# First modulation wholly on TensorE, gate1 loads earlier, paired head products, filler products

## The chip, the cores and the metric

The kernel runs on one core of one Trainium2 chip. The metric is device time in microseconds (us). Before the change three runs gave a median of 1546.49 us (1546.27 to 1547.13).

## What is computed

One layer of a hybrid encoder block on x of 512 tokens by 1024 channels, float32, with one conditioning vector c:

```python
mod = silu(c) @ w_ada + b_ada
shift1, scale1, gate1, shift2, scale2, gate2 = split(mod, 6)
h = rms_norm(x) * (1 + scale1) + shift1
q, k, v, zg = split(h @ w_in)
attn = windowed_gqa(q, k, v, sink)        # 8 heads, 2 kv heads, blocks of 128, band of 3 blocks
u, vg = split(gelu(zg), 2)
gm = u * (W_s @ layer_norm(vg) + b_s)     # per chunk of 128 tokens, 8 channel groups
mix = concat(rms_norm(attn), rms_norm(gm))
x = x + gate1 * rms_norm(mix @ w_out)
h2 = rms_norm(x) * (1 + scale2) + shift2
# expert choice: 16 experts, each takes its 64 best tokens of softmax(h2 @ w_router)
out_e = (silu(xs @ w_gate) * (xs @ w_up)) @ w_down   # 1024 -> 2816 -> 1024, times the gate
x = x + gate2 * rms_norm(scatter_add(out_e))
```

The three expert weights are 16 x 3 x 11.5 MB = 554 MB and are read once.

## The kernel before

The program has two parts. The **mixing part** computes everything up to the routing; the **expert part** runs sixteen experts one after the other on weights that stream from HBM. All transfers are issued on SP's queue, in program order, and an issue that must wait for its buffer holds up all issues behind it. The Tile framework's planner puts each engine's instructions in an order at build time; on the chip each engine then runs its own list strictly in that order.

Stages of the mixing part, in program order:

- **Loads**: small vectors, x, then eight `wq` chunks of 1.4 MB, one for each block of 128 channels: the columns of `w_ada` for shift1 and scale1 of these channels, and the rows of `w_in` for q, k, v.
- **x**: squares on ScalarE, 32 transposes (`x_cols`), 1/rms with `rsqrt` (a guess from the bits and three Newton steps on VectorE, eight instructions for a single column), 1/rms as a row (`x_norm`, `rxb`).
- **q, k, v**: the order of `SEQ`, with `m` = the first modulation's shift1 and scale1 of a channel block, `d` = `modulate` (two VectorE passes and one on ScalarE give h in two float32r parts), `q` = `qkv` (18 products of 512 columns into the six banks `qkp`). For the blocks in `MODPE` (0, 1, 2, 3, 5) `m` is `mod1_rows`, 32 products on TensorE; for blocks 4, 6 and 7 it is `mod1_acc`, eight VectorE passes, and `mod1_cols` at `d` finishes it with a few products.
- **g units**: eight `unit("g", k)` of 12 products, for the gMLP's v half. Beside them `mod2(0, *)` and `mod2(1, *)`: each `mod2(i, kk)` loads 1 MB of `w_ada` into a slot and adds two row tiles to `racc` with two VectorE passes (L553, L555); i = 0 is gate1, 1 shift2, 2 scale2, 3 gate2. `mod2_cols(i)` then makes columns on TensorE, and for gate1 spreads it over 128 rows (`G0`, 16 products).
- **u units**: eight `unit("u", k)`, for the u half. Beside them `mod2_cols(0)`, `mod2_cols(1)`, `mod2(2, *)`, and `gate_norm(b)` for each token block: layer norm of v, with an `rsqrt` of its own, then two GpSimd passes.
- **steps** (`at_step`, one for a head pair of a block): `attn_scores`, two steps later `attn_out`, which transposes the probabilities of heads j and j + 4 and multiplies them with v, 128 columns to a product (L462, two to six products a head); the spatial gating, the split of `w_out` into two parts (`out_weights`, L656/L657), the output projection (`project`, `project_z`), `residual`, then for each token block `x2_cols`, `logits`, `affinity`, and for the last block the routing of the first expert (`rank_part`, `route(0)`). `gate2` (step `GS` = 23) spreads gate2 over 128 rows.

Expert chunks go to buffers that the mixing part frees: six slots, three buffers that held `wz` (parts of `w_out`, last read by `project_z(3, 1)`), three that lie where the attention's tiles were, one where `ow` was, and places. The loads of the first expert's weights wait for them (L835).

The six slots also hold `wq`, `ada2`, `wst`, part of `wi` and `wo`. `load_gu("u", 0)` goes to a place that `xT` held and so waits for the last `modulate`.

Of the kernel before, what the change touches and what calls it, by code (L numbers as in the profile page):

```python
# [7 lines left out]
F32 = mybir.dt.float32  # L8
# [6 lines left out]
P = 128  # L15
# [9 lines left out]
NE = 16  # L25
# [22 lines left out]
TINY = 2.0 ** -126  # L48


@with_exitstack
def encoder_block(ctx, tc, x, c, w_ada, b_ada, norm_pre_mix, norm_post_mix, w_in, sink, sgu_ln_g,
# [32 lines left out]
    # ---------------------------------------------------------------- loads  # L85
# [17 lines left out]
    # columns of w_ada for shift1, scale1 of 128 channels with the rows of w_in for q, k, v of these channels  # L103
# [18 lines left out]
    def more_loads():  # L122
# [15 lines left out]
        nc.sync.dma_start(lnb, sgu_ln_b.to_broadcast([P, DG]))  # L138
        wst = slot([NG, P], name="wst")
# [4 lines left out]
    # ---------------------------------------------------------------- constants  # L144
# [24 lines left out]
    def make_dist():  # L169
        """|distance|, or a huge number outside the window; keys in front of, of, behind the block"""  # L170
# [10 lines left out]
    def rsqrt(dst, v, n):  # L181
        """dst = 1/sqrt(v) for [P, n] f32, to f32's accuracy: a guess from the bits, then Newton."""
        i = rs.tile([P, n], I32, name="rs_i", tag=f"rs_i{min(n, 2)}", bufs=2 if n == 1 else 1)
        nc.vector.tensor_scalar(i, v.bitcast(I32), -0.5, float(0x5F3759DF), op0=OP.mult, op1=OP.add)
        h = rs.tile([P, n], F32, name="rs_h", tag=f"rs_h{min(n, 2)}", bufs=2 if n == 1 else 1)
        nc.vector.tensor_scalar(h, v, -0.5, None, op0=OP.mult)
        y = i.bitcast(F32)
        t = rs.tile([P, n], F32, name="rs_t", tag=f"rs_t{min(n, 2)}", bufs=2 if n == 1 else 1)
        for r in range(3):
# [5 lines left out]
            o = dst if r == 2 else rs.tile([P, n], F32, name="rs_y", tag=f"rs_y{min(n, 2)}")  # L195
            nc.vector.scalar_tensor_tensor(o, t, 1.5, y, op0=OP.add, op1=OP.mult)
            y = o
# [29 lines left out]

    param_cols(0, np0)
# [8 lines left out]
    # ---------------------------------------------------------------- x: transposed; 1 / rms  # L237
# [29 lines left out]
    # ---------------------------------------------------------------- shift1, scale1; h  # L267
# [7 lines left out]
    def mod_rows(pm, col, w, n, first, last):  # L275
        """w [P, 4, n]: four column tiles of the array add col^T w at once"""
# [4 lines left out]
    def mod_cols(rows, n):  # L281
        """the four rows of rows [P, n] as columns: [P, n / 128, 4] in PSUM"""
# [5 lines left out]
    def mod1_rows(k):  # L288
        """PE: even and odd rows of w_ada in column tiles of their own"""
# [17 lines left out]
    acc1 = {}  # L307

    def mod1_acc(k):
        """DVE: the sums over a partition's rows"""  # L310
        acc1[k] = t = ea.tile([P, 2, P], F32, name="acc1", bufs=2)
        for kk in range(KD):
            w = wq[k][0][:, :, kk]
            if kk == 0:
                nc.vector.tensor_scalar(t, w, cs[:, kk:kk + 1], None, op0=OP.mult)
            else:
                nc.vector.scalar_tensor_tensor(t, w, cs[:, kk:kk + 1], t, op0=OP.mult, op1=OP.add)  # L317

    def mod1_cols(k):
        pm = bank("pm")  # L320
        for j in range(2):
            nc.tensor.matmul(pm[32 * j:32 * j + 32, :P], ones.to_broadcast([P, 32]), acc1[k][:, j], start=True,
                             stop=True, tile_position=(0, 32 * j))
        rows = rs.tile([P, P], F32, name="rows", bufs=1)[:64]
        nc.vector.tensor_copy(rows, pm[:64, :P])
        pt = bank("pt")
        nc.tensor.transpose(pt[:, :64], rows, ident[:64, :64])
        mod1_end(k, pt[:, 0:1], pt[:, 32:33])

# [6 lines left out]
    # ---------------------------------------------------------------- input projection  # L336
# [3 lines left out]
    def split(hi, lo, src):  # L340
        """src as a sum of two parts that float32r holds"""
# [10 lines left out]
    def qkv(k):  # L352
        """heads j and j + 4 of q share a block of rows; then k, v"""
# [10 lines left out]

    for b in range(NB):
        sumsq(ssx[:, b:b + 1], x_sb[:, b], junk)
        if b == NB - 1:
            x_rsqrt(b, NB)
        x_cols(b)
        if b == NB - 2:  # L370
            x_rsqrt(0, b + 1)
    def emit(what, k):
        if what == "m":
            (mod1_rows if k in MODPE else mod1_acc)(k)
        elif what == "d":
            if k not in MODPE:
                mod1_cols(k)
            modulate(k)
        elif what == "q":
            if k == KD - 1:  # L380
# [5 lines left out]
                load_gu("g", 0)  # L386
            qkv(k)
            if k == 0:
                more_loads()
                load_gu("g", 1)  # L390

# [49 lines left out]

    def attn_out(n, j):
        """the same heads' outputs, transposed"""
        k0, k1 = max(0, n - 1), min(NB, n + 2)
        w = (k1 - k0) * P
        if j == 0 or (n, j) == (NB - 1, 3):
            po[n, j] = bank("po")
        else:
            po[n, j] = po[n, 0]
        pT = []  # L450
        for g in range(2):
            pt = bank("ptr")
            for i in range(k1 - k0):
                nc.tensor.transpose(pt[:, i * P:(i + 1) * P], probs[n, j][:, g, i * P:(i + 1) * P], ident)
            pT.append(at.tile([P, 3 * P], F32, name="pT", tag="pT", bufs=4))
# [629 lines left out]
```

## Time and profile before

| | us |
|---|---|
| median of three runs | 1546.49 |
| span of the profiled execution | 1544.5 |
| first expert product (L949) begins | 266.5 |
| TensorE busy in the span | 1387.1 |
| VectorE busy in the span | 429.7 |

The page names 596.86 MB of transfers, 386 GB/s over the span. No execution time of the profiled run is given apart from its span, which is 2.0 us under the median of the runs. [...]

### The profile page before, as it was taken

Reading aid. Unit: us, or ns where it says so; the run is one execution under the profiler, and the core shown is the slowest. Engines: PE = TensorE matmul, PEld = TensorE weight load, DVE = VectorE, ACT = ScalarE, POOL = GpSimd, SP = SyncE. Lnnn points to the kernel's source line nnn. Section 1 sums busy time; section 2 is a strip of 40 time slices with the busy share of each in tenths; the row PEclk is TensorE's granted clock in tenths of the full one; section 3 lists DMA queues with packets and bytes.
Section 4 is the critical chain, followed back from the end, with each engine's and each line's share of the span. In section 5 each row is a group of like instructions: output and inputs, shape, how many; then the busy total and the mean of one; then the engine's idle time right before and its main releaser. Section 6 shows DMA issues by size and latency. Waiting matters only on the chain.

```text
span 1544.5 us, 17570 instructions
## 1 busy us (share of the span) xinstructions
PE 1387.1 (90%) x7282; PEld 619.8 (40%) x7282; DVE 429.7 (28%) x1087; ACT 188.9 (12%) x404; POOL 116.0 (8%) x144
## 2 busy tenths in 40 slices
PE   7888998999999998998898998989898989898986
PEld 5665665343444433333333333324242423333323
DVE  5789857112112120212112111112020303020104
ACT  3336433000010000000100000000000000000001
POOL 2457310000000000000000000000000000000002
PEclk9998999999999999999999999999999999999998
DMA  9776608999999999999999999999999999999995
GB/s 316 275 252 181 241 6 334 415 411 428 429 429 429 429 429 428 429 428 429 429 428 429 429 429 429 429 428 429 429 428 429 429 429 429 428 429 429 429 396 202
DMA packets 92711, 596.86 MB, mean 386 GB/s; under 512 B 8692, under 2 KB 31960, under 8 KB 44760
## 3 DMA queue, kind: packets, MB, share of 16 engines
q1 hardware_dynamic: 92632, 595.74, 93.3%
q8 instruction: 57, 0.93, 0.2%
q14 instruction: 22, 0.18, 0.0%
HBM read 593.62 MB, written 2.10 MB: 386 GB/s over the span
## 4 chain that ended last, share of the span: by engine, by line
DMA 60%; PE 28%; DVE 8%; issue 1%; ACT 1%; POOL 1%; SPq 0%; DVEq 0%; ACTq 0%; POOLq 0%
DMA w<-in_w_down_dram 23%; DMA w<-in_w_up_dram 19%; DMA w<-in_w_gate_dram 18%; PE pf L949 11%; PE pd L991 4%; PE px L888 1%; PE pys L1001 1%; PE py L348 1%; PE py L346 1%; PE po L462 1%; PE py L347 1%; DVE ex L851 1%; PE pd L1031 1%; DVE racc L555 1%; DVE acc L317 1%
## 5 line engine op out<-in xcount | busy, mean ns | idle before, releaser
L949 PE MATMUL pf<-w,ex 128*64 128x512 f32 (+1 forms) x3072 | 638.0, 561 | 42.0 <-DMA w<-in_w_up_dram 40.6
L949 PEld LDWEIGHTS pf<-w,ex 128*64 128x64 f32 x3072 | 215.0, 137 | 433.2 <-issue 326.2
L991 PE MATMUL pd<-w,ex 128*64 128x512 f32 (+1 forms) x1440 | 319.3, 563 | 33.7 <-DMA w<-in_w_down_dram 33.7
L991 PEld LDWEIGHTS pd<-w,ex 128*64 128x64 f32 x1440 | 109.9, 136 | 231.7 <-issue 126.0
L967 DVE TENSOR_TENSOR ex<-pf,ex 128x512 f32<-128x512 f32 (+1 forms) x48 | 30.4, 647 | 362.3 <-PE pf L949 362.0
L995 DVE TENSOR_SCALAR ex<-pd,gc 128x512 f32<-128x512 f32 x15 | 11.3, 751 | 377.6 <-PE pd L991 377.6
L907 POOL COPY ex<-ex 128x512 f32<-128x512 f32 x16 | 9.8, 613 | 1138.2 <-DVE ex L905 1058.0
L888 PE MATMUL px<-x_sb,ex 128*64 128x256 f32 x512 | 71.0, 386 | 8.6 <-DVE ex L864 7.4
L919 ACT ACTIVATE ex<-pot 128x512 f32<-128x512 f32 x16 | 9.6, 597 | 544.6 <-PE pot L917 544.6
L1007 DVE TENSOR_TENSOR y<-pys,y 128x512 f32<-128x512 f32 x112 | 68.2, 681 | 17.0 <-PE pys L1001 17.0
L974 ACT ACTIVATE ex<-pht 128x512 f32<-128x512 f32 (+1 forms) x48 | 23.5, 559 | 374.6 <-PE pht L973 374.6
L1001 PE MATMUL pys<-ex 64*128 64x512 f32 x240 | 55.6, 602 | 12.7 <-DVE ex L995 12.7
L900 DVE TENSOR_SCALAR ex<-pxt,mods 128x64 f32<-128x64 f32 x128 | 34.9, 337 | 92.0 <-PE pxt L895 92.0
L888 PEld LDWEIGHTS px<-x_sb,ex 128*64 128x64 f32 x512 | 41.3, 136 | 38.3 <-DVE ex L864 18.8
L851 DVE SCALAR_TENSOR_TENSOR ex<-rt,afs,before 128x512 f32<-128x512 f32 (+2 forms) x65 | 46.8, 719 | 12.3 <-PE rt L858 12.3
L913 DVE COPY gc<-pgc 128x1 f32<-128x1 f32 x16 | 2.5, 158 | 152.6 <-PE pgc L910 152.6
L555 DVE SCALAR_TENSOR_TENSOR racc<-ada,cs,racc 128x1024 f32<-128x1024 f32 x28 | 42.6, 1521 | 0.2
L959 ACT ACTIVATE ex<-pf 128x512 f32<-128x512 f32 (+1 forms) x48 | 26.9, 561 | 121.2 <-PE pf L949 120.4
L1001 PEld LDWEIGHTS pys<-ex 64*128 64x128 f32 x240 | 21.9, 186 | 47.1 <-DVE ex L995 25.9
L973 PE MATMUL pht<-ident,ex 128*128 128x128 f32 x176 | 25.7, 295 | 12.1 <-DVE ex L967 12.1
L973 PEld LDWEIGHTS pht<-ident,ex 128*128 128x128 f32 x176 | 22.7, 213 | 22.7 <-DVE ex L967 22.7
L890 ACT ACTIVATE ex<-px 128x256 f32<-128x256 f32 x32 | 12.3, 383 | 125.7 <-PE px L888 125.6
(254 smaller groups left out, 1086.3 us busy)
## 6 DMA issues: line engine op xcount, KB each, us to landing
w<-in_w_gate_dram SPq DMA_DIRECT2D x128, 1408.0 KB, 26.8
w<-in_w_up_dram SPq DMA_DIRECT2D x126, 1408.0 KB, 26.8
w<-in_w_down_dram SPq DMA_DIRECT2D x120, 1408.0 KB, 26.8
ada<-in_w_ada_dram SPq DMA_DIRECT2D x16, 1024.0 KB, 6.5
w<-in_w_down_dram SPq DMA_DIRECT2D x18, 512.0 KB, 9.6
wq<-in_w_ada_dram SPq DMA_DIRECT2D x16, 512.0 KB, 5.9
wi<-in_w_in_dram SPq DMA_DIRECT2D x4, 1024.0 KB, 5.2
wq<-in_w_in_dram SPq DMA_DIRECT2D x8, 384.0 KB, 6.2
```

The source lines that it names most:

```text
L555: nc.vector.scalar_tensor_tensor(acc[i], t[:, r], cs[:, k:k + 1], acc[i], op0=OP.mult, op1=OP.add)
L851: nc.vector.scalar_tensor_tensor(junk[:, :c1 - c0], p[:, c0:c1], afs[:, b, e:e + 1], before[:, o + c0:o + c1], op0=OP.subtract, op1=OP.is_ ...
L888: nc.tensor.matmul(px[i][h * CAP:(h + 1) * CAP, :256], ohr[:, b], x_sb[:, b, c0:c0 + 256], start=(b == 0), stop=(b == NB - 1))
L900: nc.vector.tensor_scalar(xs[:, k], pt[:, c0:c0 + CAP], s2[:, k:k + 1], sh2[:, k:k + 1], op0=OP.mult, op1=OP.add)
L949: nc.tensor.matmul(pb[n][h * 64:(h + 1) * 64, :NW[n]], XS[e][:, k], t, start=(i == 0), stop=(i == KD - 1))
L959: nc.scalar.activation(hid[:, n * 512:n * 512 + NW[n]], pg[n][:, :NW[n]], AF.Silu)
L967: nc.vector.tensor_tensor(hs, pu[n][:, :NW[n]], hs, op=OP.mult)
L973: nc.tensor.transpose(p[:, j * P:(j + 1) * P], hv[:, j0 + j], ident)
L974: nc.scalar.activation(hT[:, j0:j0 + n], p.rearrange("p (j t) -> p j t", j=4)[:, :n], AF.Copy)
L991: nc.tensor.matmul(pd[dh * 64:(dh + 1) * 64, c0:c0 + n], hT[:, j, h * CAP:(h + 1) * CAP], t[:, o - q * FF:o - q * FF + n], start=(h == 0 a ...
L1001: nc.tensor.matmul(p, OT[e][dh * 64:(dh + 1) * 64, b * P:(b + 1) * P], oe[dh * 64:(dh + 1) * 64, :], start=True, stop=True)
L1007: nc.vector.tensor_tensor(yb, p, yb, op=OP.add)
```

## The change

- `mod1_acc`, `mod1_cols` and `MODPE` go; `mod1_rows` does all eight blocks.
- In `SEQ` gate1's four loads and eight VectorE passes (`a0` to `a3`) stand among the last `m`, `d`, `q`; the g loop then takes `mod2(1, *)` and `mod2(2, *)`, with `mod2_cols(0)` after g unit 2; `mod2_cols(1)` and `mod2_cols(2)` stand in the u loop after units 0 and 3. gate2's loads stay at steps 8 and 9, its columns go from step 10 to 11. `M2` and `GN` go.
- `load_wst` is moved behind `q2`, `load_gu("g", 0)` from `q7` to `q3`, `load_gu("g", 1)` from `q0` to `q6`.
- `attn_out` gathers heads j and j + 1 in one `pT` tile per group and multiplies both at once, 256 columns to a product, at odd j. `pT` has two buffers of twice the size, where it had four.
- `rsqrt` takes minus half of its argument and has one third-order step and one Newton step: six instructions for one column, eight for several (eight and eleven before). The callers form minus half of the argument in an instruction that they had already. `x_rsqrt` runs once for all four blocks; `gate_norm` runs once, with one `rsqrt` of four columns.
- `keep_warm`: products into a bank that nobody reads: six of 512 columns ahead of `param_cols(0)`; for the last token block one of 256 behind each half of `x2_cols`, three of 256 behind `logits`; four of 128 in `route(0)`.
- `gate2` moves from step 23 to 20. The last block's projection is cut 2 + 2 heads where it was 3 + 1.

```diff
-MODPE = (0, 1, 2, 3, 5)
-SEQ = "d0 m1 q0 d1 m2 d2 m3 q1 d3 m4 q2 d4 m5 q3 d5 m6 q4 d6 m7 q5 d7 q6 q7"
-M2 = (0, 0, 1, 1, 3)
-M3 = (8, 8, 9, 9, 10)
-GN = (None, None, 0, 0)
-GS, RS = 23, 21
+SEQ = "d0 m1 q0 d1 m2 d2 m3 q1 d3 m4 q2 d4 m5 q3 d5 m6 q4 d6 m7 a0 q5 d7 a1 q6 a2 q7 a3"
+M3 = (8, 8, 9, 9, 11)
+GS, RS = 20, 21
...
-    def rsqrt(dst, v, n):
+    def rsqrt(dst, h, n):
         i = rs.tile([P, n], I32, name="rs_i", tag=f"rs_i{min(n, 2)}", bufs=2 if n == 1 else 1)
-        nc.vector.tensor_scalar(i, v.bitcast(I32), -0.5, float(0x5F3759DF), op0=OP.mult, op1=OP.add)
-        h = rs.tile([P, n], F32, name="rs_h", tag=f"rs_h{min(n, 2)}", bufs=2 if n == 1 else 1)
-        nc.vector.tensor_scalar(h, v, -0.5, None, op0=OP.mult)
+        nc.vector.tensor_scalar(i, h.bitcast(I32), -0.5, GUESS, op0=OP.mult, op1=OP.add)
...
+        square()
+        p = rs.tile([P, n], F32, name="rs_p", tag=f"rs_y{min(n, 2)}")
+        nc.vector.scalar_tensor_tensor(p, t, 5 / 3 / ALPHA ** 2, t, op0=OP.add, op1=OP.mult)
+        z = rs.tile([P, n], F32, name="rs_y", tag=f"rs_y{min(n, 2)}")
+        nc.vector.scalar_tensor_tensor(z, p, 1.25 / ALPHA ** 4, y, op0=OP.add, op1=OP.mult)
+        y = z
+        square()
+        nc.vector.scalar_tensor_tensor(dst, t, 1.5, y, op0=OP.add, op1=OP.mult)
...
+    def keep_warm(w, data, n):
+        p = bank("warm")
+        for _ in range(n):
+            nc.tensor.matmul(p[:, :data.shape[1]], w, data, start=True, stop=True)
+
+    keep_warm(before[:, :P], before[:, :S], 6)
     param_cols(0, np0)
...
         if what == "m":
-            (mod1_rows if k in MODPE else mod1_acc)(k)
+            mod1_rows(k)
         elif what == "d":
-            if k not in MODPE:
-                mod1_cols(k)
             modulate(k)
...
+            elif k == 2:
+                load_wst()
+            elif k == 3:
+                load_gu("g", 0)
+            elif k == 6:
                 load_gu("g", 1)
+        else:
+            mod2(0, k)
...
         for g in range(2):
+            if j % 2 == 0:
+                pTs[g] = at.tile([P, 3, 2, P], F32, name="pT", tag="pT", bufs=2)
             pt = bank("ptr")
...
+        if j % 2:
+            for i in range(nk):
+                for g in range(2):
+                    nc.tensor.matmul(po[n, j][g * HD:(g + 1) * HD, (j - 1) * P:(j + 1) * P],
+                                     v_sb[:, k0 + i, g * HD:(g + 1) * HD], pTs[g][:, i].rearrange("p j q -> p (j q)"),
+                                     start=(i == 0), stop=(i == nk - 1))
...
-        mod2(k // 4, k % 4)
+        mod2(1 + k // 4, k % 4)
+        if k == 2:
+            mod2_cols(0)
...
-        if k < 2:
-            mod2_cols(k)
-        if GN[k] is None:
-            gate_norm(k)
+        if k in (0, 3):
+            mod2_cols(1 + k // 3)
+        if k == 0:
+            gate_norm()
```

## Rows read from the trace of the kernel before

**Rows 1.** The page's 40 slices of the span: DMA busy, in tenths.
```profile
DMA  9776608999999999999999999999999999999995
```
**Rows 2.** Windows by stage: fields as told under the profile before.
```profile
16.00:70.00 54.00, 47.69 (x304) 34.90 (x304) 34.84 (x71) 17.73 (x31) 18.78 (x24) 0.91 0.87 282
70.00:93.50 23.50, 23.32 (x102) 18.54 (x102) 15.91 (x12) 7.19 (x12) 15.15 (x10) 1.00 0.97 355
93.50:131.00 37.50, 32.72 (x152) 22.53 (x150) 37.30 (x77) 13.56 (x26) 22.79 (x16) 0.91 0.63 193
131.00:154.50 23.50, 17.92 (x161) 10.71 (x161) 21.16 (x49) 17.98 (x39) 16.30 (x20) 0.91 0.57 176
154.50:231.80 77.30, 74.86 (x433) 53.05 (x432) 53.75 (x176) 31.33 (x82) 16.88 (x27) 0.94 0.34 123
231.80:247.40 15.60, 15.43 (x95) 11.44 (x94) 11.23 (x48) 7.18 (x21) 0.93 (x2) 1.00 0.99 403
247.40:266.60 19.20, 11.94 (x103) 8.41 (x104) 14.37 (x67) 6.60 (x18) 0.61 (x1) 0.91 0.72 284
266.60:1522.00 1255.40, 1146.77 (x5824) 448.23 (x5824) 221.15 (x528) 75.20 (x151) 14.22 (x19) 1.00 1.01 425
```
**Rows 3.** Waits of SP's queue, 184 to 233 us: us in total, times, longest.
```profile
SPq L835 <- PE py L348: 49.2, 2, 48.8
```
**Rows 4.** Waits of TensorE, 0 to 266 us, same columns.
```profile
PE pm L322 <- DVE acc L317: 4.5, 2, 2.6
PE ptr L454 <- DVE am L432: 4.1, 2, 3.7
...
PE po L462 <- ACT pT L459: 3.2, 7, 1.4
...
PE pm L278 <- DVE racc L555: 2.8, 1, 2.8
```
**Rows 5.** Timeline of VectorE: start, us, instruction; x's rsqrt, then `residual`'s.
```profile
12.61 0.14 DVE L258 TENSOR_SCALAR ssx<-ssx 128x1 f32<-128x1 f32 x1
...
15.77 0.68 DVE L196 SCALAR_TENSOR_TENSOR rx<-rs_t,rs_y 128x1 f32<-128x1 f32 x1
...
250.18 0.15 DVE L184 TENSOR_SCALAR rs_i<-vv 128x1 int32<-128x1 int32 x1
...
251.74 0.16 DVE L196 SCALAR_TENSOR_TENSOR rr<-rs_t,rs_y 128x1 f32<-128x1 f32 x1
```
**Rows 6.** Timeline of TensorE: the first modulation's two forms; idle time and releaser in brackets.
```profile
41.30 0.41 PE L322 MATMUL pm<-acc,ones 128*32 128x128 f32 x4 [1.90 <-DVE acc L317]
...
42.74 1.08 PE L293 MATMUL pm<-wq,cs 128*32 128x128 f32 x32
```
**Rows 7.** Windows of 4 us around the second fall of the clock, fields as in Rows 2.
```profile
52.00:56.00 4.00, 2.27 (x10) 1.46 (x11) 3.46 (x11) 0.00 (x0) 0.26 (x1) 0.86 1.06 406
56.00:60.00 4.00, 4.00 (x15) 3.17 (x13) 2.67 (x6) 1.49 (x3) 0.74 (x1) 0.71 0.96 387
```
**Rows 8.** Waits of SP's queue, 40 to 64 us.
```profile
SPq L119 <- DVE t L332: 11.5, 1, 11.5
```
**Rows 9.** Timeline of VectorE: passes of `mod2` beside the g units and later.
```profile
74.73 13.73 DVE L555 SCALAR_TENSOR_TENSOR racc<-ada,cs,racc 128x1024 f32<-128x1024 f32 x7
...
166.59 1.27 DVE L555 SCALAR_TENSOR_TENSOR racc<-ada,cs,racc 128x1024 f32<-128x1024 f32 x1
```
**Rows 10.** Timeline of TensorE: head outputs, and the routing at the end of the part.
```profile
207.36 0.87 PE L462 MATMUL po<-pT,v_sb 128*64 128x128 f32 x10
...
220.54 0.66 PE L462 MATMUL po<-pT,v_sb 128*64 128x128 f32 x8 [1.45 <-ACT pT L459]
...
252.83 1.93 PE L712 MATMUL ph<-ident,x_sb 128*128 128x128 f32 x8 [3.79 <-DVE x_sb L698]
...
258.25 2.03 PE L585 MATMUL spr<-ident,mods 128*128 128x128 f32 x16
...
261.63 4.06 PE L888 MATMUL px<-x_sb,ex 128*64 128x256 f32 x32 [1.24 <-DVE rank L872]
```

More of the change, by code (lines that the diff above doesn't have):

```diff
@@ L305, in mod1_end @@
         nc.vector.tensor_tensor(sh1[:, k:k + 1], shift, pcol("ba", k), op=OP.add)
[L307 to L328, printed above, removed]
     def modulate(k):
@@ L363, in qkv, with mod2 @@
             mm3(qkp[m], h[:, c0:c0 + P], l[:, c0:c0 + P], hh[k], hl[k], k == 0, k == KD - 1)
+    G0 = cp.tile([P, D], F32, name="G0")
+    mods = cp.tile([P, 4, 8], F32, name="mods")
+    g1c, sh2, s2, g2c = (mods[:, i] for i in range(4))
+    rb = cp.tile([P, NE], F32, name="rb")
+    acc = {}
+    def mod2(i, kk):
+        t = slot([2, D], name="ada2")
+        nc.sync.dma_start(t, ada[:, 2 * kk:2 * kk + 2, 2 + i])
+        if kk == 0:
+            acc[i] = (ea if i < 2 else at).tile([P, D], F32, name="racc")
+        for r in range(2):
+            k = 2 * kk + r
+            if k == 0:
+                nc.vector.tensor_scalar(acc[i], t[:, r], cs[:, k:k + 1], None, op0=OP.mult)
+            else:
+                nc.vector.scalar_tensor_tensor(acc[i], t[:, r], cs[:, k:k + 1], acc[i], op0=OP.mult, op1=OP.add)
@@ new lines, in mod2_cols @@
+    def mod2_cols(i):
+        pm = bank("pm2")
+        mod_rows(pm, ones, acc[i].rearrange("p (j w) -> p j w", j=4), 256, True, True)
+        rows = at.tile([P, 256], F32, name="rows2", tag="pT", bufs=2)
+        nc.vector.tensor_copy(rows, pm[:, :256])
+        m = mod_cols(rows, 256)
+        nc.vector.tensor_tensor(mods[:, i].rearrange("p (j q) -> p q j", j=4), m,
+                                pcol("ba", 16 + 8 * i, 8).rearrange("p (j q) -> p q j", j=4), op=OP.add)
+        if i == 0:
+            nc.vector.tensor_tensor(g1c, g1c, pcol("pom", 0, 8), op=OP.mult)
+            spread(G0, g1c)
+        elif i == 2:
+            nc.vector.tensor_tensor(s2, s2, pcol("npf", 0, 8), op=OP.mult)
+            pb = bank("pb")
+            for k in range(KD):
+                mod_rows(pb, sh2[:, k:k + 1], wr[:, k:k + 1].to_broadcast([P, 4, NE]), NE, k == 0, k == KD - 1)
+            nc.vector.tensor_scalar(rb, pb[:, :NE], -1.0, None, op0=OP.mult)
+            nc.vector.scalar_tensor_tensor(wsp[:, :, :NE], wr, -1.0, s2.unsqueeze(2).to_broadcast([P, KD, NE]),
+                                           op0=OP.mult, op1=OP.mult)
+        elif i == 3:
+            nc.vector.tensor_tensor(g2c, g2c, pcol("pof", 0, 8), op=OP.mult)
@@ L365, in encoder_block, with spread @@
+    def spread(dst, cols):
+        for i in range(2):
+            p = bank("spr")
+            for k in range(4):
+                kk = i * 4 + k
+                nc.tensor.matmul(p[:, k * P:(k + 1) * P], cols[:, kk:kk + 1].to_broadcast([P, P]), ident,
+                                 start=True, stop=True)
+            nc.scalar.activation(dst[:, i * 512:(i + 1) * 512], p, AF.Copy)
     for b in range(NB):
@@ L534, in gmlp_cols @@
         nc.vector.tensor_tensor(ml, p, mh.bitcast(F32), op=OP.subtract)
-    G0 = cp.tile([P, D], F32, name="G0")
-    mods = cp.tile([P, 4, 8], F32, name="mods")
-    g1c, sh2, s2, g2c = (mods[:, i] for i in range(4))
-    rb = cp.tile([P, NE], F32, name="rb")
-    acc = {}
-    def mod2(i, kk):
-        t = slot([2, D], name="ada2")
-        nc.sync.dma_start(t, ada[:, 2 * kk:2 * kk + 2, 2 + i])
-        if kk == 0:
-            acc[i] = (ea if i < 2 else at).tile([P, D], F32, name="racc")
-        for r in range(2):
-            k = 2 * kk + r
-            if k == 0:
-                nc.vector.tensor_scalar(acc[i], t[:, r], cs[:, k:k + 1], None, op0=OP.mult)
-            else:
-                nc.vector.scalar_tensor_tensor(acc[i], t[:, r], cs[:, k:k + 1], acc[i], op0=OP.mult, op1=OP.add)
@@ L579, in spread @@
-    def spread(dst, cols):
-        for i in range(2):
-            p = bank("spr")
-            for k in range(4):
-                kk = i * 4 + k
-                nc.tensor.matmul(p[:, k * P:(k + 1) * P], cols[:, kk:kk + 1].to_broadcast([P, P]), ident,
-                                 start=True, stop=True)
-            nc.scalar.activation(dst[:, i * 512:(i + 1) * 512], p, AF.Copy)
     pacc = {}
@@ L764, in encoder_block @@
         at_step(OWS[k], (out_weights, k))
-        at_step(M2[k], (mod2, 2, k))
         at_step(M3[k], (mod2, 3, k))
-    at_step(M2[4], (mod2_cols, 2))
     at_step(M3[4], (mod2_cols, 3))
-    for k in range(4):
-        if GN[k] is not None:
-            at_step(GN[k], (gate_norm, k))
     at_step(5, (gmlp_var,))
```

123 lines of the change are left out of this document (47 added, 76 removed).

## The prediction

> **What bounds the kernel now.** I read the page's slices first, then windows by stage, then the waits of SP and of TensorE. The DMA engines are busy to the end from slice 7 on, and idle only ahead of it [rows 1]. From 266.6 to 1522 us they stay at 425 GB/s while TensorE is busy 1146.8 of 1255.4 us [rows 2]: the expert part is a weight stream, and none of the edits touches it. What can move is the time at which the stream runs free. In the mixing part SP waits 48.8 us for the last products with `wz` [rows 3], because all other buffers are full; the rest of the buffers follow from attention and routing. So I take the end to be the time of the first expert product plus a constant, and every us that the mixing part loses is an us off the kernel. Before 180 us there is DMA room too (share 0.57 to 0.97 [rows 2]).
>
> The mixing part is bound by TensorE, but not everywhere by its work. Two losses can be read from [rows 2] for each stage: its idle time (length minus busy) and what half clock costs (length x (1 - granted clock), if it worked throughout). 16 to 70 us (q, k, v): 6.3 and 4.9. 70 to 93.5 (g units): 0.2 and 0. 93.5 to 131 (u units): 4.8 and 3.4, with VectorE busy 37.30 of 37.50 us, so VectorE is the bound there. 131 to 154.5 (spatial gating, parts of w_out): 5.6 and 2.1. 154.5 to 247.4 (attention, projection): 2.6 and 4.6. 247.4 to 266.6 (routing): 7.3 and 1.7. Some 43 us in all; the change goes for most of them.
>
> **q, k, v.** *Removed:* the passes of `mod1_acc`, for which TensorE waits 4.5 us in two waits [rows 4], and the fall of the clock behind the second: 4 x (0.14 + 0.29) = 1.7 us [rows 7]. *Added:* three times a form of 1.08 us instead of 0.41 [rows 6], 2.0 us of TensorE's own time. Of the 4.5 I take 3.5, since a chain m, copy, transpose, d, q remains. x's two interleaved rsqrts take 3.84 us from 12.61 to 16.45; eight instructions took 1.72 us in `residual` [rows 5], so 0.215 each, and nine in a row take 1.9: at most 1.9 earlier, I take 1.5, as wq's first modulation ends about then. The first fall of the clock, soon after x, I leave as it is; the six fillers stand well ahead of it, and run while TensorE has nothing else. Sum: 1.5 + 3.5 + 1.7 - 2.0 = **4.7**, between 1 and 9 (all waits and both falls gone).
>
> *Moved:* gate1's eight passes come beside q, k, v, where VectorE loses 24 passes of `mod1_acc`; it has room (34.84 of 54 us [rows 2]). Its loads pass, in SP's queue, the load of `wi` that waited 11.5 us for the last `modulate` [rows 8] and had held three of them and all of the others back. `wst` and both `wi` of the g half still stand ahead of their first use by several us. On VectorE the passes stand in line: a pass that waits for its 1 MB holds `d7` behind `a0` only, the copies of k and v behind `a3`. All loads up to 154.5 us are about 35 MB by [rows 2] (54 x 282 + 23.5 x 355 + 37.5 x 193 + 23.5 x 176 MB/1000); in 16 us less that is some 285 GB/s, which the stages before have shown.
>
> **g and u units.** Sixteen passes (`mod2(1, *)`, `mod2(2, *)`) leave the u stage for the g stage: at 1.27 us alone [rows 9] 20 us of the 37.3 that bound it. TensorE's 30 us then bound it; POOL's 22.8 [rows 2] fit. Its wait for `racc` (2.8 us [rows 4]), the other idle time and the fall behind it go: 8.2, less 1.5 for waits behind copies: **6.7**, between 3 and 8.2. `mod2_cols(0)` costs TensorE the same in either loop. `gate_norm` in one piece starts when the last gelu is done and has all u units as cover; without that cover its GpSimd passes (some 13 us) would hold `spatial`.
>
> **Spatial gating, parts of w_out.** The longest wait here (3.7 us [rows 4]) stands behind VectorE's low parts of w_out, which cannot start before the spatial gating has freed the memory. The change leaves that. Only the waits ahead of it lose their backlog: **2.2** of 7.7, between 0 and 7.7.
>
> **Paired heads.** Eight products take 0.66 us, 0.082 each, at 128 columns [rows 10]. No trace row shows this product at 256; the nearest is `px`, 256 columns and 64 weights: 4.06 / 32 = 0.127. A pair with three key blocks has 12 products before (0.98) and 6 after (0.76), one with two 8 (0.66) and 4 (0.51): 4 x 0.22 + 4 x 0.15 = 1.5. Half of the seven waits for copies (3.2 us [rows 4]) fall away: 1.6. Together **3.1**; if 256 columns cost twice 128 and the copies wait for the fewer buffers, 0; if the falls of the clock in this stage go as well, 7.7. [...]
>
> **Routing.** `residual`'s rsqrt loses two of eight instructions: 0.43 us; the one of `x2_cols` half of that, as other work stands between. Eight transposes took 1.93 us at half clock [rows 10]; with gate2's 16 products ahead of them in the 3.79 us gap, and the fillers, they may take half: 0.97. The spread no longer stands ahead of the routing's transposes: 0.35. Sum **2.0**; fillers that run when the next operand is ready already cost up to 1 (3 x 0.127 to 0.254, and the shorter ones), so from -1 to 3.5.
>
> **Sum.** 4.7 + 6.7 + 2.2 + 3.1 + 2.0 = 18.7 us. Span 1544.5 - 18.7 = 1525.8; the median stood 2.0 over the span, so 1527.8 us. VectorE's shorter rsqrts elsewhere cost and bring nothing: TensorE covers them.
>
> **The rivals.** *More goes.* If the whole loss of the spatial stage and the half clock of the attention stage vanish, 5.5 + 4.6 more: 1517.7. For it: each fall follows a wait; against it: the wait for w_out's parts has no cause that the change removes.
>
> *VectorE and GpSimd crowd the g stage.* Beside the g units seven passes took 13.73 us, 1.96 each, later one took 1.27 [rows 9]; POOL is busy 15.15 us there [rows 2]. Sixteen passes at 1.27 and POOL's 15.15, if they exclude each other, need 35.5 us; the stage has 23.5 + 3.4. The splits come late, TensorE waits 8.6 us: 1536.4. Against it: VectorE's and POOL's busy time there sum to 31 in 23.5 us already, and TensorE hardly waits. [...]
>
> *The two buffers of `pT` (slower).* A pair's first copy must wait for the products of the pair ahead, and these for its last copy. If the planner leaves nothing between, each pair shows the wait of 1.45 us [rows 10] for both heads and a fall like the one of 1.7 [rows 7]: 4.6 us a pair, eight pairs 36.8, no pairing gain: 1527.8 + 3.1 + 36.8 = 1567.7. It makes the kernel slower from four pairs on (15.6 / 4.6). Against it: projections stand between pairs, as they do now.
>
> *It does not do what it says.* The lists are planned anew; if VectorE's list has loads' passes ahead of what TensorE needs, waits for loads take the place of those for passes, and nothing is won: 1546.5.
>
> **How the numbers follow.** A measurement of this kernel can tell about 0.2% (3 us) from no change. Forecast 0.60, more 0.14, crowding 0.14, no gain 0.05, slower 0.07. Faster 0.60 + 0.14 + 0.14 = 0.88, same 0.05, slower 0.07. The range reaches from just under the larger gain (1516) to past the crowding (1539); the terms' own lower ends, if several come together, reach there too. It leaves out slower and no gain, and the far ends.
>
> **What would show it.** q, k, v: the last `qkp` product about 5 us before 69.6, no wait for `acc`. u stage: about 31 us or less, VectorE under 0.7 busy. Attention: L462 groups of 256 columns, 6 products near 0.8 us. First expert product near 248 us, the DMA share 1.0 behind it as now. The forecast is wrong if TensorE waits for VectorE behind a load in the g stage, if the clock falls more often, or if the first expert product moves and the end does not.

## The result, and the profile after

| | before | after |
|---|---|---|
| median of four runs, us | 1546.49 | 1558.85 (1557.73 to 1559.59) |
| span of the profiled execution, us | 1544.5 | 1557.0 |
| first expert product begins, us | 266.5 | 267.3 |
| from there to the end of the span, us | 1278.0 | 1289.7 |

The kernel became slower: ratio 1.0077, 95% interval 1.0065 to 1.0089. The prediction, 1527.8 with a range from 1516 to 1539, was wrong twice over. The mixing part, which was to end 18.7 us earlier, ends 0.8 us later; and the expert part, which was to keep its length, takes 11.7 us more. (Left out of the times below are two executions at a far lower clock: the profiled one of e6, at a mean of 0.75, whose trace is not read, and one of e1, at 0.56.)

Windows by stage of the kernel after, cut where its own stages end (q, k, v; g units; u units; spatial gating up to the first product of a projection; attention and projection in two; routing; experts). The fields, here and in [rows 2], are the stretch, its length, busy time (and instructions) of TensorE, of its weight loads, of VectorE, ScalarE and GpSimd, the granted clock of TensorE (1.00 is full speed, 0.50 half clock), the mean busy share of the DMA engines, and GB/s:

```profile
16.00:66.90 50.90, 49.46 (x421) 37.70 (x421) 24.30 (x57) 19.43 (x34) 21.81 (x26) 0.90 1.00 301
66.90:94.50 27.60, 26.28 (x128) 20.52 (x129) 20.57 (x19) 8.04 (x13) 13.92 (x9) 1.00 1.03 403
94.50:138.00 43.50, 31.90 (x205) 22.29 (x203) 33.10 (x59) 12.92 (x26) 27.84 (x22) 0.88 0.54 159
138.00:155.40 17.40, 11.22 (x56) 6.91 (x56) 14.34 (x26) 15.14 (x32) 9.96 (x11) 0.91 0.25 80
155.40:232.00 76.60, 73.36 (x394) 49.45 (x392) 54.73 (x168) 33.68 (x90) 16.39 (x28) 0.98 0.38 140
232.00:247.80 15.80, 14.59 (x82) 10.64 (x86) 9.63 (x37) 6.53 (x22) 0.94 (x2) 1.00 0.88 357
247.80:267.30 19.50, 14.86 (x120) 10.96 (x119) 13.90 (x63) 5.90 (x18) 0.61 (x1) 0.91 0.61 243
267.30:1522.00 1254.70, 1138.20 (x5761) 440.92 (x5762) 216.75 (x521) 72.45 (x143) 9.20 (x15) 1.00 1.01 422
```

Beside [rows 2], q, k, v end 3.1 us earlier. The g units take 4.1 us more, as `mod2_cols(0)` and its spread now stand there, at full clock (1.00). The u units take 43.5 us where 31 were forecast, with TensorE busy for 31.90; `mod2_cols(2)` now stands among them. The spatial stage takes 17.4 us where it took 23.5, with 56 TensorE instructions in it for 161. In the last row the DMA engines are as busy as before (1.01), but they move 422 GB/s, not 425.

TensorE's waits from 0 to 266 us (us in total, times, longest), beside [rows 4]:

```profile
PE pu L325 <- POOL wl L321: 10.7, 1, 10.7
PE po L499 <- ACT pT L495: 5.3, 8, 1.5
PE ptr L490 <- DVE am L465: 4.3, 1, 4.3
PE warm L226 <- POOL before L158: 3.9, 1, 3.9
PE b L250 <- DVE pc L220: 2.4, 1, 2.4
PE ph L702 <- DVE x_sb L688: 2.1, 1, 2.1
```

The waits for `acc` and `racc` are gone, as forecast. In their place stand one of 10.7 us for GpSimd in the u units, one of 2.4 for `pc` at the start, and more for `pT`. The wait of the spatial stage has stayed (3.7 in [rows 4], 4.3 now).

Two timelines show the 10.7 us (start, us, instruction; in brackets idle time and releaser). GpSimd's, then TensorE's:

```profile
109.03 2.28 POOL L548 TENSOR_TENSOR vn<-vn,sgu 128x512 f32<-128x512 f32 x1
111.28 3.67 POOL L547 TENSOR_TENSOR vn<-vn,sgu 128x512 f32<-128x512 f32 x2
114.91 4.44 POOL L548 TENSOR_TENSOR vn<-vn,sgu 128x512 f32<-128x512 f32 x2
119.31 2.24 POOL L547 TENSOR_TENSOR vn<-vn,sgu 128x512 f32<-128x512 f32 x1
121.51 2.24 POOL L321 TENSOR_TENSOR wl<-wi,wh 128x512 fp32r<-128x512 f32 x1
```

```profile
112.71 0.40 PE L324 MATMUL pu<-wh,hh 128*128 128x512 f32 x1
123.81 0.80 PE L325 MATMUL pu<-wl,hh 128*128 128x512 f32 x1 [10.70 <-POOL wl L321]
124.40 0.63 PE L326 MATMUL pu<-wh,hl 128*128 128x512 f32 x1
```

Six passes of `gate_norm` (L547, L548) run in one block on GpSimd; the split of the next unit's weights (L321) stands behind them in its list. TensorE stops at 112.7 us, goes on at 123.8, and its products then take 0.63 us instead of 0.40: half clock (granted 0.50 from 123.8 to 128 us, 1.00 from 112 to 113).

### The profile page after: what moved, and what is told of

The parts are those of the page before. It is cut to its first block, busy times and chain, and to the rows that moved or that the text cites. A ratio compares the mean times of both kernels' runs of the same rounds, so it can differ in the third digit from the quotient of the medians.

```text
span 1557.0 us, 17542 instructions
## 1 busy us (share of the span) xinstructions
PE 1388.6 (89%) x7310; PEld 615.6 (40%) x7310; DVE 407.4 (26%) x997; ACT 188.1 (12%) x404; POOL 114.7 (7%) x144
## 3 DMA queue, kind: packets, MB, share of 16 engines
q1 hardware_dynamic: 92632, 595.74, 93.5%
## 4 chain that ended last, share of the span: by engine, by line
DMA 69%; PE 22%; DVE 4%; ACT 2%; POOL 1%; issue 1%; SPq 1%; DVEq 0%; ACTq 0%; POOLq 0%
DMA w<-in_w_down_dram 25%; DMA w<-in_w_up_dram 23%; DMA w<-in_w_gate_dram 21%; PE pf L939 6%; PE pd L981 3%; PE px L878 1%; PE qkp L324 1%; PE po L499 1%; PE pd L1021 1%; PE py L324 1%; PE py L326 1%; PE py L325 1%; PE qkp L325 1%; PE qkp L326 1%; PE pys L991 1%
## 5 line engine op out<-in xcount | busy, mean ns | idle before, releaser
L985 DVE TENSOR_SCALAR ex<-pd,gc 128x512 f32<-128x512 f32 x15 | 11.3, 751 | 383.4 <-PE pd L981 383.4
L362 DVE SCALAR_TENSOR_TENSOR racc<-ada,cs,racc 128x1024 f32<-128x1024 f32 x28 | 46.5, 1661 | 0.4
## 6 DMA issues: line engine op xcount, KB each, us to landing
w<-in_w_gate_dram SPq DMA_DIRECT2D x128, 1408.0 KB, 27.1
w<-in_w_up_dram SPq DMA_DIRECT2D x126, 1408.0 KB, 27.1
```

The lines of the kernel that those rows point to most:

```text
L362: nc.vector.scalar_tensor_tensor(acc[i], t[:, r], cs[:, k:k + 1], acc[i], op0=OP.mult, op1=OP.add)
```

## Experiments: where the stream's buffers begin

The expert part of after has the same instructions in the same order as before, so I compared what the built programs place where. The pool `rs` shrank from 2320 to 2192 bytes: `rsqrt` has lost the tile `rs_h`, three buffers of 32 bytes, and gate norm in one piece needs 32 bytes less for its small tiles. The pools `sl`, `s2p` and `s4p` lie behind it: ten of the stream's thirteen buffers begin 128 bytes lower, the first at 78720 instead of 78848, which is 154 x 512. The three of `s3p` have not moved. A buffer's size, 11264 bytes, is 22 x 512, so the ten share one offset.

**e1**, after with the old beginnings; no instruction moves:

```diff
-    rs = ctx.enter_context(tc.tile_pool(name="rs", bufs=2))
+    rs = ctx.enter_context(tc.tile_pool(name="rs", bufs=2)); rs.tile([P, 32], F32, name="pad", bufs=1)
```

> The changed kernel with one edit: 128 unused bytes in the pool rs, so that all buffers of the weight stream behind it begin where they did before the change (78848 and so on, multiples of 512 bytes; in the changed kernel they begin 128 bytes lower, at 78720). Order of all instructions unchanged. Theory A (the beginning of a buffer in memory sets the rate at which the stream fills it): 428.5 to 429 GB/s from 300 to 1500 us where the changed kernel shows 425, first expert product unchanged near 267.3, time 1546 to 1548 us. Theory B (the rate has to do with the order of the program, or with the chip of that day): 425 GB/s and 1557 to 1560 us.

1545.46 us (median of nine), against 1547.61 for before beside it: ratio 0.9987 (0.9978 to 0.9996). First expert product at 266.1, from there to the end 1277.4 us.

**e2**, the opposite: before with the new beginnings.

```diff
-        ssf = rs.tile([P, 3, NB], F32, name="ssf")
+        ssf = rs.tile([P, 3, NB], F32, name="ssf", bufs=1)
```
(and the same for `vf` and `rf`)

> The kernel before with one edit: three small tiles that are used once get one buffer instead of two, so that the stream's buffers begin at 78720 as in the changed kernel. Order of all instructions unchanged. Theory A: 425 GB/s instead of 429 from 300 to 1500 us, first expert product at 266.5, time 1557 to 1560 us. Theory B: 429 GB/s, 1546 to 1547 us.

1558.49 us, ratio 1.0076 (1.0053 to 1.0099): the loss of the change, with none of its instructions. From the first expert product to the end it takes 1289.8 us, as after does.

**e3**, before with 64 bytes more in `rs`:

```diff
+    rs.tile([P, 16], F32, name="pad", bufs=1)
```

> The kernel before with 64 unused bytes in the pool rs: the buffers begin at 78912, which is 64 past a multiple of 512. Theory A, if any beginning off the multiple is slow: 425 GB/s or less, 1557 to 1560 us or more. Theory A, if it is the multiple of 64 bytes that counts, or theory B: 429 GB/s, 1546 to 1547 us.

1557.8 us, ratio 1.0068 (1.0052 to 1.0085), 1289.6 us from the first expert product to the end: also slow.

**e12**, after with `ssf`, `vf` and `rf` single as in e2, so that the buffers begin at 78592, 256 past a multiple of 512:

> The changed kernel with the stream's buffers at 78592 and so on, 256 past a multiple of 512 (three small tiles that are used once get one buffer instead of two). Theory A (a buffer must begin at a multiple of 512): 425 GB/s from 300 to 1500 us, packets of 11264 bytes above 422 ns, 1557 to 1560 us. Theory B (a multiple of 256 does): 427 to 429 GB/s, packets of 422 ns, 1544 to 1547 us.

1545.5 us, ratio 0.9991 (0.9980 to 1.0002): fast, 1277.5 us from the first expert product to the end. Here a multiple of 256 is enough: 429 GB/s, as in e1 (windows below).

The page's part on DMA issues tells these kernels apart. Here is its line for `w_gate` (transfers, KB each, median us from issue to landing). Of before:

```profile
w<-in_w_gate_dram SPq DMA_DIRECT2D x128, 1408.0 KB, 26.8
```

Of after:

```profile
w<-in_w_gate_dram SPq DMA_DIRECT2D x128, 1408.0 KB, 27.1
```

Of e1:

```profile
w<-in_w_gate_dram SPq DMA_DIRECT2D x128, 1408.0 KB, 26.8
```

Of e2:

```profile
w<-in_w_gate_dram SPq DMA_DIRECT2D x128, 1408.0 KB, 27.0
```

Of e3:

```profile
w<-in_w_gate_dram SPq DMA_DIRECT2D x128, 1408.0 KB, 27.1
```

Of e12:

```profile
w<-in_w_gate_dram SPq DMA_DIRECT2D x128, 1408.0 KB, 26.8
```

And the same window in the middle of the stream, fields as in [rows 2]. Of after, e2 and e3, in this order:

```profile
600.00:900.00 300.00, 267.72 (x1334) 101.27 (x1332) 52.05 (x121) 15.61 (x31) 1.84 (x3) 1.00 1.01 424
600.00:900.00 300.00, 267.77 (x1338) 101.84 (x1336) 52.97 (x122) 15.66 (x31) 1.84 (x3) 1.00 1.01 425
600.00:900.00 300.00, 267.45 (x1340) 101.93 (x1337) 54.76 (x128) 15.65 (x31) 1.84 (x3) 1.00 1.01 424
```

Of e1 and e12:

```profile
600.00:900.00 300.00, 270.16 (x1364) 103.62 (x1360) 54.66 (x128) 16.04 (x32) 2.46 (x4) 1.00 1.01 429
600.00:900.00 300.00, 270.26 (x1358) 103.33 (x1360) 54.67 (x128) 16.01 (x32) 2.47 (x4) 1.00 1.01 429
```

The busy share (1.01) is the same; only GB/s and the time to landing show the loss. Over the whole expert part it is 1289.7 against 1277.4 us, 1.0%, and that is the 12 us.

**e4**, before with the three buffers of `s3p` at multiples of 512 as well (they begin 480 past one in every other kernel here):

```diff
+    pad = ctx.enter_context(tc.tile_pool(name="pad", bufs=1, side="right")); pad.tile([P, 120], F32, name="pad")
     s3p = ctx.enter_context(tc.tile_pool(name="s3p", bufs=N3, side="right", reuse_waits="tile"))
```

> The kernel before with 480 unused bytes ahead of the pool s3p: its three buffers, which begin 480 past a multiple of 512 in both kernels, begin at multiples of 512 too. Order unchanged. Theory A: ten of the thirteen buffers off the multiple cost some 12 us, so three cost 3 to 4 us; the stream rises from 429 to 430 GB/s, and the kernel takes 1542.5 to 1544 us. Theory B: 1546 to 1547 us.

1546.95 us, ratio 0.9997 (0.9986 to 1.0008): no gain. The 3 to 4 us that I expected aren't there: three buffers off a multiple of 256 cost nothing measurable, ten cost 12 us. Theory A holds for the ten, but not as a price per buffer.

## Experiments: the mixing part

From here on e1 is the base: the change with its buffers where they were. It ran on one chip, e5 to e8 on a second, where before took 1546.33 us, and e9 to e12 on a third, where before took 1548.12. So a gain over e1 is a little uncertain, and I give it by the times and by the ratios to before.

**e5**, without the six unread products at the start:

```diff
-    keep_warm(before[:, :P], before[:, :S], 6)
```

> The changed kernel with its buffers back at multiples of 512 (as e1_after_slots_back, which is the base here: first q product 21.6 us, last one ends 64.8, first expert product 266.1, 1545.5 us), and without the six unread products ahead of param_cols(0). Theory A (with the fillers the planner puts the copy of pc behind x's rsqrt in VectorE's list, and this waits for the squares of all of x at 10.7 us, so that x's transposes stand for 2.3 us): no wait of x's transposes for pc, first q product at 19.5 to 20.5 us, last one at 63 to 64; the first expert product 1 to 2 us earlier, near 264.5, time near 1544. Theory B (the single rsqrt for all four blocks is to blame, not the fillers): the wait stays, and nothing moves by over 0.5 us. Theory C (what is won at the start is lost behind the wait for GpSimd in the u units): q products as in A, first expert product at 266.

1541.1 us, ratio 0.9970 (0.9957 to 0.9983), 4.4 us under e1 by the times and 2.6 by the ratios. Theory A holds, and more comes than it said: first q product at 19.1 us, last one done at 62.8, first expert product at 260.8. The start of TensorE's timeline, in after:

```profile
3.90 2.74 PE L226 MATMUL warm<-before 128*128 128x512 bf16 x6 [3.90 <-POOL before L158]
6.57 0.37 PE L219 MATMUL pp<-ident,prm 64*128 64x64 f32 x1
6.87 4.29 PE L250 MATMUL b<-ident,x_sb 128*128 128x128 f32 x28
13.60 0.66 PE L250 MATMUL b<-ident,x_sb 128*128 128x128 f32 x4 [2.44 <-DVE pc L220]
15.92 1.94 PE L294 MATMUL pm<-wq,cs 128*32 128x128 f32 x32 [1.67 <-issue]
```

In e5:

```profile
3.12 0.34 PE L219 MATMUL pp<-ident,prm 64*128 64x64 f32 x1 [3.12 <-DMA prm<-in_norm_pre_mix_dram]
5.54 6.48 PE L249 MATMUL b<-ident,x_sb 128*128 128x128 f32 x32 [2.09 <-DMA x_sb<-in_x_dram]
11.95 0.41 PE L293 MATMUL pm<-wq,cs 128*32 128x128 f32 x4
13.05 1.07 PE L293 MATMUL pm<-wq,cs 128*32 128x128 f32 x28 [0.69 <-DMA wq<-in_w_ada_dram]
```

And VectorE's timeline in after:

```profile
11.66 0.17 DVE L259 TENSOR_SCALAR ssx<-ssx 128x4 f32<-128x4 f32 x1 [9.59 <-ACT junk L208]
...
13.32 0.21 DVE L220 COPY pc<-pp 128x64 f32<-128x64 f32 x1
```

In e5:

```profile
3.49 0.23 DVE L220 COPY pc<-pp 128x64 f32<-128x64 f32 x1 [1.63 <-PE pp L219]
```

The fillers are not free although TensorE had nothing else to do: with them in the program, the planner puts the copy of `pc` behind x's rsqrt, which waits 9.59 us for the last squares. The copies of x's transposes stand behind it, x's last transposes wait, and the first modulation then runs at half clock (1.94 us for 32 products, granted clock 0.50; without the fillers 28 of them take 1.07 us). So behind the products that were to hold the clock stand waits of 2.44 and 1.67 us, and behind the second the clock is 0.50. From 16 us to the end of q, k, v it is 0.90 in after, 1.00 in e5.

**e6**, `gate_norm`'s column passes on VectorE:

```diff
-            nc.gpsimd.tensor_tensor(v, v, lng, op=OP.mult)
-            nc.gpsimd.tensor_tensor(v, v, lnb, op=OP.add)
+            nc.vector.tensor_tensor(v, v, lng, op=OP.mult)
+            nc.vector.tensor_tensor(v, v, lnb, op=OP.add)
```

> The same base, with the eight passes of gate_norm that multiply and add by columns on VectorE instead of GpSimd. Theory A (TensorE's 10.7 us wait in the u units is for a split that stands behind these passes in GpSimd's list, and the half clock there follows from it): the wait is gone, u units end at 124 to 127 us instead of 136.2, first expert product 6 to 10 us earlier (256 to 260), time 1536 to 1540. Theory B (VectorE takes 8 x 0.7 = 5.6 us more and is late for other work, so the wait only changes its name): u units end past 132, first expert product at 264 or later, time 1543 to 1547. Theory C (the first expert product moves and the end doesn't, since transfers bound the end): 256 to 260, but 1544 to 1546.

1539.0 us (median of four), ratio 0.9955 (0.9939 to 0.9972), 6.5 us under e1 by the times and 4.9 by the ratios: theory A's time. Its other signs can't be read here. Where the edit acts is shown by the windows of e9, which has it too.

**e7**, gate2's spread back at step 23:

```diff
-GS, RS = 20, 21
+GS, RS = 23, 21
```

> The same base, with gate2's spread at step 23 as before the change, so that its 16 products stand between the last logits and the routing's transposes; all fillers stay. Theory A (it was this spread that held the clock for the routing's 32 products px, which now take 5.36 us instead of 4.06; ten short fillers do less than it did): px in 4.1 us, clock 1.00 from 258 to 266, first expert product near 265.2; the eight ph, which now run at full clock, may fall back to half clock, +0.7. Theory B (the spread only delays the routing by what it takes behind the last logits): px still 5.4, first expert product at 266.1 to 266.5.

1546.05 us, ratio 0.9994 (0.9985 to 1.0004): as the base. Two rows of the routing on TensorE's timeline, of e1:

```profile
251.74 0.63 PE L702 MATMUL ph<-ident,x_sb 128*128 128x128 f32 x4 [2.08 <-DVE x_sb L688]
...
259.85 5.36 PE L878 MATMUL px<-x_sb,ex 128*64 128x256 f32 x32 [0.34 <-DVE rank L862]
```

Of e7:

```profile
251.37 1.09 PE L702 MATMUL ph<-ident,x_sb 128*128 128x128 f32 x4 [3.58 <-DVE x_sb L688]
...
261.52 4.07 PE L878 MATMUL px<-x_sb,ex 128*64 128x256 f32 x32 [0.34 <-DVE rank L862]
```

Theory A's signs are there, px takes 4.07 us, but so is its price: without the spread the gap ahead of `ph` is 3.58 us, and `ph` and the fillers behind it run at half clock (1.09 us for four `ph`, 0.63 in e1; 1.06 for two rows of filler, 0.60 in e9). The fall is moved, not removed, and the first expert product comes at 266.4. That the spread's place set px's clock isn't shown: after, with e1's instructions, has px in 4.06 us too.

**e8**, heads not paired (`attn_out` as in before, and the last projection cut 3 + 1):

```diff
-                pTs[g] = at.tile([P, 3, 2, P], F32, name="pT", tag="pT", bufs=2)
...
-        if j % 2:
...
+            pT.append(at.tile([P, 3 * P], F32, name="pT", tag="pT", bufs=4))
```

> The same base, with attn_out as before the change: one head per product of 128 columns, four buffers of pT. Theory A (the pairs bring what was forecast, 3.1 us): first expert product 2.5 to 3.5 us later, near 269, time 1548 to 1549. Theory B (the waits of 1.45 us for pT, which are now 5.3 us in all where they were 3.2, eat the gain of the wider products): first expert product within 0.7 us of 266.1, time as the base.

1553.97 us, ratio 1.0050 (1.0035 to 1.0065), first expert product at 275.1: 8.5 us slower and 9.0 later than e1. Both theories said too little. The first product of a projection comes at 161.0 instead of 153.7; from there to the last one it takes 93.9 us instead of 92.5. So 1.4 us lie in the stage of the products and their copies, and 7.3 ahead of it, 6.2 of them between the last product of the u units and the first of a projection (23.7 us instead of 17.5): the order of the lists differs around the spatial gating. There TensorE's timeline has, just ahead of the first projection, at half clock (eight rows in 1.12 us, 0.66 in [rows 10]):

```profile
159.99 1.12 PE L497 MATMUL po<-pT,v_sb 128*64 128x128 f32 x8 [2.79 <-ACT pT L494]
```

What in the planner makes that order was not tried.

**e9**, the edits of e5 and e6 together:

> The changed kernel with three edits at once: buffers back at multiples of 512 (e1), no six fillers at the start (e5), gate_norm's column passes on VectorE (e6). Over e1 (1545.5 us, first expert product 266.1) e5 brought 4.4 us and e6 5.6. Theory A (the two losses are separate, the gains add): first expert product 255 to 257, time 1535 to 1537. Theory B (they overlap: e5 had already cut the wait for GpSimd from 10.7 to 8.0 us, and the spatial gating's wait of 4 us for VectorE stays whatever comes before it): 258 to 260, time 1538 to 1540.

1533.9 us, ratio 0.9914 (0.9899 to 0.9928), first expert product at 256.4. Beside the base it is 11.6 us by the times, 11.3 by the ratios, where e5 and e6 sum to 10.9 and 7.5: as theory A had it, the gains add within their intervals. It is faster than both kernels of the study, than before by some 13 us. TensorE's u units and what follows them, in windows:

```profile
90.50:114.00 23.50, 23.48 (x107) 17.98 (x105) 23.05 (x36) 6.83 (x12) 8.93 (x6) 1.00 0.53 168
114.00:132.30 18.30, 13.03 (x116) 7.20 (x116) 12.64 (x38) 7.86 (x22) 5.15 (x11) 0.66 0.72 201
```

The u units now take 23.5 us without a gap. But the first attention steps and `mod2_cols(2)`, which ran among them in e1, now stand behind them alone, with TensorE busy for 13.0 of 18.3 us at a mean clock of 0.66: there more is to be had.

**e10**, four more fillers in the routing:

```diff
+        if b == NB - 1:
+            keep_warm(ident, hTs[b][:, 6:8].rearrange("p k t -> p (k t)"), 4)
```

> As e9, with four more unread products of 256 columns behind the last block's pl2, where TensorE waits 1.7 us for VectorE's aff before the routing's transposes. Theory A (this gap is why the clock falls before px): px in 4.1 us instead of 5.4, first expert product 1.0 to 1.3 us before that of e9. Theory B (four fillers at 0.52 us each take 2.1 us and overrun the wait of 1.7): the transposes start 0.3 to 0.5 later, the gain is 0.6 to 1.0 or less; if the clock falls all the same, 0.3 to 0.5 us slower than e9.

**e11**, e9 with none there:

```diff
-                keep_warm(ident, xb[:, i * S:i * S + 256], 1)
...
-            keep_warm(ident, hT[:, 6:8].rearrange("p k t -> p (k t)"), 3)
...
-            keep_warm(afs[:, NB - 1, 0:1].to_broadcast([P, P]), ident, 4)
```

> As e9, without the ten unread products of the routing (two behind the halves of x2_cols, three behind logits, four in route(0), of the last block). Theory A (they hold the clock through x2_cols): the eight ph and what follows at half clock, first expert product 1 to 2 us later than in e9. Theory B (they only shift the fall of the clock from ph to px): within 0.5 us of e9.

e10: 1533.73 us; e11: 1534.91 us (ratios 0.9911, 0.9895 to 0.9928, and 0.9919, 0.9903 to 0.9935). In e9 px already ran at full clock, 4.07 us, so e10 had nothing to gain there, and from the last projection to the first expert product both take 18.5 us: whether four more are worth it where the clock does fall is not shown. e11 takes 19.8 us for the same, with this row on TensorE's timeline:

```profile
247.72 5.50 PE L872 MATMUL px<-x_sb,ex 128*64 128x256 f32 x32 [1.23 <-DVE rank L856]
```

So beside e9 and e10 the routing is 1.3 us longer without the fillers (nine products: two, three and four). That they bring this isn't shown: between whole times, 1.0 us, the intervals overlap, there is one trace without them, and traces of one and the same list of instructions differ here by up to 1.9 us (next section). Of theory A's signs px at half clock came, for a part of it (5.50 us, 4.07 in e9), but the eight `ph` took 1.29 us, most of it at full clock (in e9 0.63 and 0.60, in [rows 10] 1.93), and the first expert product came at 254.1, ahead of e9's: this execution was 3.6 us ahead before the routing began.

## Why the prediction was wrong, step by step

**One trace is one execution.** Before, e2, e3 and e4 have the same instructions in the same order, and so have after, e1 and e12; only where buffers begin differs. Side by side they show what a difference between two traces can be worth (us, from TensorE's timelines, in the order of the names):

| | before, e2, e3, e4 | after, e1, e12 | e9, e10, e11 |
|---|---|---|---|
| last q, k, v product ends | 70.0, 69.5, 70.5, 71.0 | 66.9, 64.8, 65.7 | 63.5, 62.2, 62.5 |
| from there to the first projection product | 84.4, 84.4, 84.4, 84.4 | 88.6, 88.9, 89.2 | 80.9, 81.0, 79.5 |
| from there to the end of the last one | 93.1, 92.1, 89.1, 89.3 | 92.3, 92.5, 92.6 | 93.4, 93.5, 92.3 |
| from there to the first expert product | 19.0, 20.9, 20.8, 20.9 | 19.5, 19.8, 19.8 | 18.5, 18.5, 19.8 |

**"The end is the time of the first expert product plus a constant"; "none of the edits touches" the expert part.** This is the step that turned the sign. The constant is one: 1278.0 in before, and 1276.5 to 1278.1 in e1, e5, e7, e8, e9, e10, e11 and e12, whose first expert products lie between 254 and 275 us. But the edits did touch it. The smaller working sets of `rsqrt` and gate norm moved ten buffers off a multiple of 256 bytes, and the constant became 1289.7. The prediction went through instructions, waits and queues, and left out what an edit of a pool does to the addresses behind it; the diff showed the tiles that go. By e1 this cost 13.4 us of the 1558.85.

**Gate norm in one piece, costed at nothing.** The cover was named, "all u units", with what its loss would cost, "some 13 us". The step failed in what the passes hold up: not `spatial` behind the u units, but the u units' own splits, which are on the same engine. TensorE waited 10.7 us, and the half clock behind it may have cost up to 5 more (43.5 x 0.12, an estimate from the window above). From the last q, k, v product to the end of the u units before took 61.0 us, after 71.1. Part of these 10.1 us is work that stood behind the u units before, and the spatial stage became shorter, so the sum of the three stages tells more: 84.4 us before, 88.6 after. The terms of the g and u units and of spatial gating, 6.7 and 2.2 to the good, came out 4.2 to the bad together. e9, e10 and e11 are the check from the other side: with these passes on VectorE, and without the fillers at the start, it is 79.5 to 81.0.

The rival "VectorE and GpSimd crowd" had part of this. Passes of `racc` that stand beside those of `gate_norm` take 2.2 us each, against 1.27 alone in [rows 9]:

```profile
111.52 11.11 DVE L362 SCALAR_TENSOR_TENSOR racc<-ada,cs,racc 128x1024 f32<-128x1024 f32 x5
```

The passes of GpSimd take some 2.2 too, where the last of the eight, alone at 123.7 us, took 1.27. Six at 1.27 would be 7.6 us, an estimate; in the block they took 12.5. The rival was placed in the g units, where TensorE hardly waits (26.28 of 27.60 us busy), and it priced late splits at 8.6 us; they cost 10.7, one stage on. The trace shows both sides longer at once. In e9, where GpSimd has nothing to do from 107.9 to 124.0 us, the five passes of `racc` from 108.3 to 115.4 us take 1.27 each. Why both are longer side by side is not shown.

**Fillers that "run while TensorE has nothing else".** True of the engine, not of the planner: e5 puts their harm at 2.6 to 4.4 us. The forecast for the last q, k, v product was 4.7 earlier, 9 at best. In the mean of the traces in the table it comes 4.5 earlier, 7.5 without the fillers (with e5, 62.8). That the sum was met is luck: the fillers took some 3 that it put at nothing, and the other edits of this term brought as much more than it said.

**Paired heads, 3.1.** The mechanism held, the count didn't. In the trace each of these products has two rows, so eight rows, 0.66 us in [rows 10], are one head with two key blocks and not a pair. (The 32 of px are rows too: the prices were taken by the row and the counts by the product.) With pairs, eight rows of 256 columns, of after:

```profile
232.96 1.08 PE L499 MATMUL po<-pT,v_sb 128*64 128x256 f32 x8 [1.44 <-ACT pT L495]
```

That is 0.135 each, near the 0.127 taken from px. A pair with two key blocks then saves 1.32 - 1.08 = 0.24 instead of 0.15, one with three 0.36 instead of 0.22 (an estimate from the same rows), and all eight 2.4 instead of 1.5. The waits for `pT` did not halve, they grew from 3.2 to 5.3 us, as the slower rival feared, but without its fall of the clock at each pair (0.98 and 1.00 in the stage's two windows). In the whole stage the term doesn't show: 92.3 to 92.6 us, against 89.1 to 93.1 for the list of before. e8 gives 1.4 us for the stage and 7.3 for the order of the lists; none of the rows of before that the prediction read tells the second.

**Routing, 2.0.** After, it takes 19.5 us from the last projection product, before 19.0. But before's own trace was a lucky one: gate2's spread, which stood behind the last logits there, took 2.03 us at full clock in [rows 10], and 3.6 to 3.7 in e2, e3 and e4. Of e2:

```profile
256.90 3.74 PE L585 MATMUL spr<-ident,mods 128*128 128x128 f32 x16
```

By the middle values of the table, 20.8 and 19.8, the change brings 1.0 of the 2.0. In e9, where the clock held (the eight `ph` 0.63 and 0.60 us, px 4.07), the routing takes 18.5.

**Spatial gating, 2.2.** The wait for VectorE's low parts of `w_out` stayed, as argued (3.7, then 4.3; in e9 3.4, ahead of the projection). That the stage is 6 us shorter all the same goes with `mod2_cols(2)`, which left it, and, by e8, with the pairs and the order of the lists that comes with them.

**The balance.** 1558.85 less 13.4 (e1) less 11.6 (e9) is 1533.9, still 6 us above the forecast. By stage, e9's trace against before's: q, k, v 6.5 earlier (4.7 forecast), the three stages up to the first projection product 3.5 shorter (8.9), attention and projection 0.3 longer (3.1 shorter), routing 0.5 shorter (2.0).

## What to carry to other kernels

When an edit changes what a pool holds, list where the buffers behind it begin, before and after, and pad them back, here to a multiple of 256 bytes. In a kernel bound by one stream look at GB/s and at the time a transfer takes: the busy share of the DMA engines was 1.01 with the slower stream (424 GB/s, 27.1 us) and with the faster (429, 26.8). Before a difference of 1 or 2 us between two traces is explained, look for a second trace of the same instructions. For work that is gathered into one block, name every other user of that engine's list in the same stretch, not only the block's own reader; and treat an unread product as an instruction that the planner sees, which can reorder other engines.

## What the runs showed of the hardware

**Where its buffers begin sets the rate of this saturated stream.** With ten of thirteen buffers at offsets 64 (e3) or 128 (after, e2) past a multiple of 256 the stream ran at 424 to 425 GB/s, at offset 0 of 256 (e1, also 256 of 512 in e12) at 429, with the DMA engines' busy share at 1.01 in all of them. Over the expert part that is 1.0%. By what the beginning sets the rate is not shown. Nor is e4 explained: three buffers that begin off the multiple cost nothing beside ten that don't, and it stays open whether the loss sets in at some share of such buffers.

**The clock's falls move, also between executions of the same instructions.** After, e1 and e12 have the same list: in after the half clock hit what stands behind `ph` (granted 0.57 from 254.7 to 258.6 us; px 4.06 us at 1.00), in e1 and e12 px (5.36 us). In before's list it spared gate2's spread in one trace (2.03 us, granted clock 1.00) and hit them in three (3.60 to 3.74). With the same routing fillers it hit `ph` in e7 (1.09 us for four) and nothing in e9 (0.63, px 4.07). What a filler is worth in a place can't be read from one trace.
